# Cross-entropy backward on one core: the stores of second rows move from ACT's queue to Pool's

## The chip, the cores and the metric

The kernel runs on one core of a Trainium2 chip. Its engines work side by side and meet at semaphores: VectorE (DVE), ScalarE (ACT), GpSimd (Pool), SyncE (SP) and TensorE (PE). SP, ACT and Pool can issue DMAs; the data are moved by 16 DMA engines that all queues share. The metric is device time in microseconds, the median of the runs. The profile is of one further execution, and its span is the time from the first to the last instruction.

## The reference

For 8 x 1024 positions with 8192 logits each, the result is the softmax of the logits less 1.0 at the label:

```python
batch, seq_len, vocab = 8, 1024, 8192
logits_max = np.max(logits, axis=-1, keepdims=True)
exp_logits = np.exp(logits - logits_max)
softmax = exp_logits / np.sum(exp_logits, axis=-1, keepdims=True)
...
return (softmax - one_hot).astype(np.float32)
```

Input and output are 268.4 MB each in fp32; each is moved once.

## The kernel before

**Rows and blocks.** The 8192 positions are cut into T = 64 tiles of 128 positions, one to a partition; the code calls such a tile a row, t. A row is 128 x 8192 fp32, 32 KB on each partition, 4 MB. Two rows (G = 2) make a block, b = 0 to 31: row t = 2b is the block's first row (j = 0), t = 2b + 1 its second (j = 1). Both lie next to each other in memory on every partition. X holds SLOTS = 3 blocks, so block b uses slot b % 3, and everything is computed in place in X.

**Loads.** `load(b)` is called three blocks ahead. The string LOADS says in what pieces a block comes: "s" (blocks 0 to 2) in four half rows of 64 partitions, two of them on ACT's queue, "r" (blocks 3, 4 and 29 to 31) in two rows, "w" (blocks 5 to 28) as a whole block, 64 KB on each partition. All but the halves named are issued by SP. A load waits until the stores of block b - 3 that it would overwrite have landed: a row's load for that row's store, a block's load for both.

**One row.** `row_max(t)` on DVE (tensor_reduce, m) waits for the load. `exponentials(t)` on ACT takes exp and the sum s. `mark(t)`, two ACT operations, writes into PSUM (hot) a word that is 1 in the byte of the label. `finish(t)` on DVE takes the reciprocal r and then one scalar_tensor_tensor: X times r, less the bytes of hot. `store(t)` sends the row out. Each needs only what is named here, and `mark(t)` that `finish(t - 2)` has read hot.

**The order around a store.** It is written out by hand and is the same for all blocks. DVE does max(t1), finish(t0), max of the next block's first row, finish(t1). ACT does exp(t1), store(t0), mark(t0 + 2), exp of the next block's first row, store(t1), mark(t1 + 2). ACT executes its list in order, so an issue that waits for DVE holds what stands behind it. `store(t)` waits for DVE's count of `finish(t)`. All stores of blocks 0 to 30 are whole rows and are issued by ACT, each with a semaphore of its own for slot and row (`put`). The last block's two rows go out in halves of 4096 columns, row 62 by SP and row 63 by ACT. After the loop ACT waits for the landing of the last three blocks' stores.

**Pool** does four small fills, then an identity matrix and an iota for the marks, all at the start.

**Line numbers.** All instructions of the kernel are made by the helper `run` and have its line, L76 in the kernel before (L75 is its wait). In the changed kernel these are one more.

Of the kernel before, what the change touches and what calls it, by code (L numbers as in the profile page):

```python
# [9 lines left out]
SLOTS = 3  # L10
# [7 lines left out]
def kernel(  # L18
# [6 lines left out]
    nc = tc.nc  # L25
# [38 lines left out]
    with tc.tile_critical():  # L64
        sem = tc.alloc_semaphore
        got = [[sem(f"got{i}{q}") for q in range(4)] for i in range(SLOTS)]
        put = [[sem(f"put{i}{q}") for q in range(4)] for i in range(SLOTS)]
        lab_got, dve, act, pe, pool = (sem(n) for n in ("lab_got", "dve", "act", "pe", "pool"))
        count = {}

        def run(engine, waits, counter, method, **operands):

            waits = list(dict.fromkeys(waits))
            for w in waits[:-1]:
                engine.wait_ge(*w)  # L75
            instruction = getattr(engine, method)(**operands)  # L76
            for w in waits[-1:]:
                instruction._wait_ge(*w)
            step = 16 if method == "dma_start" else 1
            instruction.then_inc(counter, step)  # L80
            count[counter.name] = count.get(counter.name, 0) + step
            return counter, count[counter.name]
# [16 lines left out]
        maxed, summed, marked, finished, freed = {}, {}, {}, {}, {}  # L99
# [14 lines left out]
        def store(t):  # L114
            b, j = divmod(t, G)
            stored.setdefault(b, [])
            if t >= T - G:
                for i, cs in enumerate(sides):
                    w = run(
                        nc.sync if t == T - G else nc.scalar, [sides_done[t][i]], put[b % SLOTS][G * j + i],  # L120
                        "dma_start", out=o_b[b, every, one[j], cs], in_=X[every, b % SLOTS, one[j], cs],
                    )
                    stored[b].append(((every, one[j]), w))
                return
            for q, piece in enumerate(PIECES[STORES[b]]):
                ps, js = piece
                if js.stop != j + 1:
                    continue
                w = run(
                    nc.scalar, [finished[t]], put[b % SLOTS][q], "dma_start",  # L130
                    out=o_b[b, ps, js, :], in_=X[ps, b % SLOTS, js, :],
                )
                stored[b].append((piece, w))
# [110 lines left out]
        for b in range(B):  # L244
            t0, t1 = b * G, b * G + 1
            nxt = t1 + 1
            if ORDER[b] == "b":
                if t0 not in maxed:
                    row_max(t0)
                    exponentials(t0)  # L250
                row_max(t1)
                exponentials(t1)
                finish(t0)
                store(t0)
                mark(t0 + G)
                finish(t1)
                store(t1)
                mark(t1 + G)
                if b + SLOTS < B:
                    load(b + SLOTS)  # L260
                continue
# [4 lines left out]
            finish(t0)  # L266
            exponentials(t1)
            store(t0)
            mark(t0 + G)
            ahead = nxt < T and ORDER[b + 1] == "r"  # L270
# [42 lines left out]
```

## Time and profile before

| | |
|---|---|
| median of 3 runs | 1248.87 us (1248.83 to 1249.43) |
| span of the profiled execution | 1246.6 us |
| DVE busy | 1120.2 us |
| ACT busy | 722.7 us |
| Pool busy | 2.3 us |
| DVE idle, ended by a load | 105.4 us |
| HBM read, written | 268.50 MB, 268.44 MB |

In the profile an instruction's row gives its start and its time in us, the engine, the line, the operation and its tiles (out<-in). "ACTq" and "SPq" are the instructions with which ACT and SP issue DMAs; their time is that of the issue, and the transfer itself appears as a time to landing. Part 2 of the page cuts the span into 40 slices and gives busy shares in tenths. Part 3 gives for each DMA queue its packets, its megabytes and its share of the 16 engines' time: q10 is ACT's queue and q1 is SP's. A window is a stretch of the span with the busy time of each engine and the share of time that the DMA engines worked in it.

### The profile page before, as it was taken

How to read it: one execution, taken by the hardware profiler on the slowest of the kernel's cores; microseconds unless marked ns; L12 is line 12 of the kernel's file. 1: busy time of each engine (PE TensorE's matmuls, PEld its weight loads, DVE VectorE, ACT ScalarE, POOL GpSimd, SP SyncE). 2: the span in 40 equal slices, each digit the busy share in tenths (PEclk: the TensorE clock that was granted, in tenths of full speed). 3: DMA queues.
4: the chain of work that ended last, by engine and by line, in shares of the span. 5: the costliest groups of instructions: out<-in, count | busy, mean ns of one | idle time of the engine just before them, and what ended most of it. 6: DMA issues, size and time to landing. Idle time of an engine off the chain costs nothing.

```text
span 1246.6 us, 809 instructions
## 1 busy us (share of the span) xinstructions
PE 0.4 (0%) x2; PEld 0.3 (0%) x2; DVE 1120.2 (90%) x208; ACT 722.7 (58%) x257; POOL 2.3 (0%) x7
## 2 busy tenths in 40 slices
PE   0000000000000000000000000000000000000000
PEld 0000000000000000000000000000000000000000
DVE  5999998889988889888898888998889988899995
ACT  2866664556555565465655655556556555566662
POOL 0000000000000000000000000000000000000000
DMA  9999999999999999999999999999999999999998
GB/s 406 413 431 434 437 432 444 435 437 421 433 429 437 443 423 433 434 431 435 430 441 435 422 435 435 434 440 426 432 434 431 433 446 434 422 430 435 429 434 383
DMA packets 15413, 536.98 MB, mean 431 GB/s; under 512 B 1808, under 2 KB 1808, under 8 KB 1840
## 3 DMA queue, kind: packets, MB, share of 16 engines
q10 hardware_dynamic: 9744, 276.89, 51.5%
q1 hardware_dynamic: 5664, 260.05, 48.3%
q14 instruction: 5, 0.04, 0.0%
HBM read 268.50 MB, written 268.44 MB: 431 GB/s over the span
## 4 chain that ended last, share of the span: by engine, by line
DMA 59%; DVE 26%; issue 11%; ACT 3%; DVEq 0%; ACTq 0%; SPq 0%
DMA X<-in_logits_dram 33%; DMA out_dram<-X 26%; DVE X L76 15%; DVE m L76 10%; ACT X L76 2%; DVEq L64 0%; DVE r L76 0%; ACT hot L76 0%; ACT away L76 0%; ACTq L76 0%; DVEq L75 0%; ACTq L308 0%; SPq L64 0%
## 5 line engine op out<-in xcount | busy, mean ns | idle before, releaser
L76 ACT ACTIVATE X<-X,m 128x8192 f32<-128x8192 f32 x64 | 455.8, 7122 | 365.2 <-DVE m L76 365.2
L76 DVE TENSOR_REDUCE m<-X 128x1 f32<-128x8192 f32 x64 | 555.6, 8682 | 105.4 <-DMA X<-in_logits_dram 105.4
L76 DVE SCALAR_TENSOR_TENSOR X<-X,r,hot 128x8192 f32<-128x8192 f32 (+1 forms) x66 | 560.1, 8489 | 3.8 <-ACT hot L76 1.6
L76 ACT ACTIVATE away<-count,word 128x2048 bf16<-128x2048 int16 x64 | 128.1, 2001 | 127.0 <-DVE X L76 127.0
L76 ACT ACTIVATE hot<-away,unit,minus 128x2048 int32<-128x2048 bf16 x64 | 131.9, 2061 | 2.1
L76 ACT ACTIVATION_READ_ACCUMULATOR X<-X,m 128x1 f32 x64 | 11.9, 186 | 0.0
L76 DVE RECIPROCAL r<-s 128x1 f32<-128x1 f32 x64 | 9.8, 153 | 0.0
L76 ACT ACT_TABLE_LOAD x1 | 1.3, 1283 | 5.3 <-issue 5.3
L76 DVE CAST lab_f<-lab_raw 32x256 f32<-32x256 int32 x1 | 0.5, 536 | 2.7 <-DMA lab_raw<-in_labels_dram 2.7
L76 POOL IOTA count<- 128x2048 int16 x1 | 1.8, 1823 | 0.0
L76 DVE TENSOR_TENSOR unit<-unit,part 128x64 f32<-128x64 f32 x3 | 0.7, 225 | 0.1
L76 DVE CAST lab<-hot 128x64 int32<-128x64 f32 x1 | 0.2, 224 | 0.5 <-PE hot L76 0.5
L76 DVE TENSOR_SCALAR part<-minus 128x64 f32<-128x64 f32 x3 | 0.6, 194 | 0.1
L76 PE MATMUL hot<-ident,lab_f 32*128 32x32 f32 x2 | 0.4, 298 | 3.3 <-DVE lab_f L76 3.3
L76 PEld LDWEIGHTS hot<-ident,lab_f 32*128 32x128 f32 x2 | 0.3, 192 | 3.3 <-DVE lab_f L76 3.3
L76 DVE CAST minus<-lab 128x64 f32<-128x64 int32 x1 | 0.2, 195 | 0.0
L76 DVE TENSOR_SCALAR word<-part 128x64 f32<-128x64 int32 x1 | 0.2, 195 | 0.0
L76 DVE TENSOR_SCALAR lab<-lab 128x64 int32<-128x64 int32 x1 | 0.2, 195 | 0.0
L76 DVE TENSOR_SCALAR unit<-minus 128x64 f32<-128x64 f32 x1 | 0.2, 195 | 0.0
L76 DVE TENSOR_SCALAR part<-lab 128x64 int32<-128x64 int32 x1 | 0.2, 194 | 0.0
L76 DVE TENSOR_SCALAR minus<-unit 128x64 f32<-128x64 f32 x1 | 0.2, 194 | 0.0
L76 POOL TENSOR_SCALAR_AFFINE_SELECT ident<-ident 32x32 f32<-32x32 f32 x1 | 0.2, 203 | 0.1
(5 smaller groups left out, 0.5 us busy)
## 6 DMA issues: line engine op xcount, KB each, us to landing
out_dram<-X ACTq DMA_DIRECT2D x62, 4096.0 KB, 30.4
X<-in_logits_dram SPq DMA_DIRECT2D x10, 4096.0 KB, 28.1
X<-in_logits_dram SPq DMA_DIRECT2D x6, 2048.0 KB, 32.6
X<-in_logits_dram ACTq DMA_DIRECT2D x6, 2048.0 KB, 37.1
out_dram<-X SPq DMA_DIRECT2D x2, 2048.0 KB, 12.7
out_dram<-X ACTq DMA_DIRECT2D x2, 2048.0 KB, 11.9
X<-in_logits_dram SPq DMA_DIRECT2D x24, 33.4
lab_raw<-in_labels_dram ACTq DMA_DIRECT2D x1, 64.0 KB, 1.8
```

The source lines that it names most:

```text
L76: instruction = getattr(engine, method)(**operands)
```

## The change

A semaphore for each slot is added, and in `store` the full second rows (j = 1) of blocks 0 to 30 are issued by Pool, with that semaphore. Pool waits for `finish(t)` as ACT did. First rows stay on ACT, the last block's halves stay on SP and ACT. The loads and the final waits of ACT use whatever semaphore the store was given. Nothing else is edited; the order of all other instructions on every engine is the same.

```diff
@@ -65,6 +65,7 @@
         got = [[sem(f"got{i}{q}") for q in range(4)] for i in range(SLOTS)]
         put = [[sem(f"put{i}{q}") for q in range(4)] for i in range(SLOTS)]
+        second = [sem(f"second{i}") for i in range(SLOTS)]
         lab_got, dve, act, pe, pool = (sem(n) for n in ("lab_got", "dve", "act", "pe", "pool"))
@@ -127,7 +128,8 @@
                 w = run(
-                    nc.scalar, [finished[t]], put[b % SLOTS][q], "dma_start",
+                    nc.gpsimd if j else nc.scalar, [finished[t]], second[b % SLOTS] if j else put[b % SLOTS][q],
+                    "dma_start",
                     out=o_b[b, ps, js, :], in_=X[ps, b % SLOTS, js, :],
                 )
```

ACT's list loses 31 DMA issues, Pool's gains 31, each of 128 x 8192 fp32, behind the iota.

## The prediction

> **What bounds the kernel now.** The page's first parts: who is busy over the whole span, and what the DMA engines carry.
>
> ```profile
> span 1246.6 us, 809 instructions
> PE 0.4 (0%) x2; PEld 0.3 (0%) x2; DVE 1120.2 (90%) x208; ACT 722.7 (58%) x257; POOL 2.3 (0%) x7
> ...
> DMA  9999999999999999999999999999999999999998
> ...
> DMA packets 15413, 536.98 MB, mean 431 GB/s; under 512 B 1808, under 2 KB 1808, under 8 KB 1840
> ...
> q10 hardware_dynamic: 9744, 276.89, 51.5%
> q1 hardware_dynamic: 5664, 260.05, 48.3%
> q14 instruction: 5, 0.04, 0.0%
> ```
>
> DVE is 90% busy, but the DMA engines are busy in every slice: the two queues, ACT's q10 and SP's q1, fill 99.8% of them. How much is idle, and where, the windows say (columns: us; busy time of PE, PEld, DVE, ACT, POOL; clock; DMA share; GB/s):
>
> ```profile
> 0.00:2.30 2.30, 0.00 (x0) 0.00 (x0) 0.00 (x0) 0.00 (x0) 1.48 (x7) 1.00 0.09 29
> 160.00:1084.00 924.00, 0.00 (x0) 0.00 (x0) 827.16 (x142) 537.92 (x192) 0.00 (x0) 1.00 1.00 433
> 1084.00:1201.70 117.70, 0.00 (x0) 0.00 (x0) 117.15 (x21) 72.89 (x26) 0.00 (x0) 1.00 1.00 433
> 1201.70:1246.60 44.90, 0.00 (x0) 0.00 (x0) 31.32 (x8) 14.51 (x6) 0.00 (x0) 1.00 0.92 397
> ```
>
> From 160 to 1084 us DVE idles 97 of 924 us while the DMA share is 1.00 at 433 GB/s: DMA is the limit there. From 1084 us DVE has no gap (117.15 of 117.70) and DMA is still full. Both end together.
>
> A floor follows: 536.98 MB at 433 GB/s is 1240.1 us. Before it stand 2.3 us with no data; behind it stands what follows the last landing. That landing is read from the end of the timeline and the DMA view of the last stores (its last number is us from issue to landing):
>
> ```profile
> 1197.79 8.75 DVE L76 SCALAR_TENSOR_TENSOR X<-X,r,hot 128x8192 f32<-128x8192 f32 x1
> 1206.45 8.68 DVE L76 TENSOR_REDUCE m<-X 128x1 f32<-128x8192 f32 x1
> ...
> 1224.22 8.87 DVE L76 SCALAR_TENSOR_TENSOR X<-X,r,hot 128x4096 f32<-128x4096 f32 x2
> 1228.73 4.73 ACTq L76 DMA_DIRECT2D out_dram<-X  x2
> ...
> out_dram<-X ACTq DMA_DIRECT2D x2, 2048.0 KB, 11.9
> ```
>
> The last half store is issued at 1233.1 us (DVE's end, 1224.22 + 8.87), lands 11.9 us later at 1245.0, and 1.6 us remain. So 1240.1 + 2.3 + 1.6 = 1244.0 us, against a span of 1246.6. No order of issue can gain more than **2.6 us** unless bytes move faster. The median of the runs, 1248.87, lies 2.3 us above the span; I add 2.3 to every span below. 0.2% is 2.5 us, about what can be told from no change.
>
> **The change part by part.** (1) 31 second-row stores leave ACT's queue, each 0.34 us of issue (the row for 1171.67 below), 10.5 us in all. ACT is 58% busy, and behind such a store stands only the pair of marks for a row that is two rows (35 us) away: worth nothing. If ACT had no room it would be 10.5 us.
>
> (2) Pool issues them. It has 2.3 us of work, whose last and longest piece starts at 1.3 us and takes 1.8 (the row below), so it stands waiting for DVE when each row is done. Nothing but the next second-row store is queued behind that wait.
>
> (3) The semaphore of its own changes no order: SP's loads and ACT's last waits ask for the same landing under another name. Zero.
>
> (4) Pool's own price is in no row. From below: zero, since other transfers keep the engines in work while one starts. From above: all 16 engines standing still for the longest issue in the trace, 657 ns, at each of 31 stores, 20 us.
>
> The rows are those of the issues and of Pool's longest instruction, by tile (ns, shortest/median/longest):
>
> ```profile
> L76 SPq DMA_DIRECT2D X<-in_logits_dram x40: 327/328/657, 1.0 to 1173.0; - x40
> ...
> L76 POOL IOTA count<- x1: 1823/1823/1823, 1.3 to 1.3; 128x2048 int16 x1
> ```
>
> I take zero, the value for work hidden under full queues, and keep 20 us for the range.
>
> (5) The real change: **three queues instead of two share the engines.** How they share now can be read from packets, with the page's part 6 (DMA issues; the last number is us to landing):
>
> ```profile
> out_dram<-X ACTq DMA_DIRECT2D x62, 4096.0 KB, 30.4
> X<-in_logits_dram SPq DMA_DIRECT2D x10, 4096.0 KB, 28.1
> X<-in_logits_dram SPq DMA_DIRECT2D x6, 2048.0 KB, 32.6
> X<-in_logits_dram ACTq DMA_DIRECT2D x6, 2048.0 KB, 37.1
> out_dram<-X SPq DMA_DIRECT2D x2, 2048.0 KB, 12.7
> ...
> X<-in_logits_dram SPq DMA_DIRECT2D x24, 33.4
> lab_raw<-in_labels_dram ACTq DMA_DIRECT2D x1, 64.0 KB, 1.8
> ```
>
> Every DMA ends in 16 small packets: with the two of 11.9 us above these are 113 DMAs, and 113 x 16 = 1808, the "under 512 B". Without these and the 5 of q14, 13,600 are left, which is the number of partition rows that these DMAs move, one packet each (62 x 128 for the stores, 24 x 128 for the block loads, and so on): 32 KB for a row's store or load, 64 KB for a block's load. And the queues take turns, packet by packet, as two neighbouring row loads in the tail show, each with its issue and its time to landing:
>
> ```profile
> 1153.66 0.33 SPq L76 DMA_DIRECT2D X<-in_logits_dram  x1
> X<-in_logits_dram SPq DMA_DIRECT2D x1, 4096.0 KB, 28.5
> ...
> 1173.00 0.33 SPq L76 DMA_DIRECT2D X<-in_logits_dram  x1
> X<-in_logits_dram SPq DMA_DIRECT2D x1, 4096.0 KB, 28.7
> ```
>
> They land at 1182.2 and 1201.7, 19.5 us apart. One row is 4.19 MB, 9.69 us at 433 GB/s; 19.5 is twice that: load and store alternate one to one. With a second store queue that has work, a row load gets a third. In the middle of the kernel this costs nothing: engines that are full stay full, and what loads lose stores gain. But stores run ahead of loads, and at the end that is the wrong way round: stores are what DMA does beside DVE's last rows.
>
> ```profile
> 1171.67 0.34 ACTq L76 DMA_DIRECT2D out_dram<-X  x1
> out_dram<-X ACTq DMA_DIRECT2D x1, 4096.0 KB, 34.8
> ...
> 1189.12 0.34 ACTq L76 DMA_DIRECT2D out_dram<-X  x1
> ```
>
> When the last load lands (1201.7), the store of 1171.67 has 4.8 us to go (it lands at 1206.5) and that of 1189.12 its full 9.69: a stock of 14.5 us, 1.5 rows. DVE was 4.75 us late for that load (its reduce starts at 1206.45): it is not waiting.
>
> How short may the way from the last landing be? DVE 1206.45 to 1233.09, 26.64 us; then the last two half stores, 9.68 us in a row, the first of which starts 4.43 us before DVE's end, so 5.25; start and landing 1.8, the time of the smallest DMA (lab_raw in part 6); and the 1.6 us after it: **35.3 us**. Before, that way takes 44.9 us, so 9.6 us of cushion; the stock pays for it.
>
> With two store queues a store starts as soon as its row is done. Alone beside a load it takes 19.4 us, and rows come 17.45 us apart (1171.67 to 1189.12), so 1.11 are under way, half done on the mean: 0.56 rows of stock. If the three always share, 29 us: 0.83. I take 0.7. The 0.8 rows that are gone were stored ahead of loads, 0.8 x 9.69 = 7.75 us. In each 17.45 us by which the last load is late, DVE adds another row that is stored ahead of it too, so the delay is 7.75 / (1 - 9.69/17.45) = 7.75 / 0.445 = 17.4 us. The last load lands at 1219.1, and the span is 1219.1 + 35.3 = 1254.4 us. With +2.3: **1256.7 us**. (At stock 0.83 it is 1254, at 0.56 it is 1260. It takes DVE's pace as unbroken in the tail; where DVE waits for loads the delay is a little smaller.)
>
> **Rivals.** *Not slower: Pool starts late, so the stock stays.* From stock 1.06 on, the delay is under the cushion of 9.6 us and nothing is lost: 1249. On the mean of all rows, stock grows by d/(2 x 17.45) for a start d us late, so 0.36 more needs d of 12.6 us. For it: what Pool needs to start a 4 MB store is unknown. Against: its longest instruction is 1.8 us. The Trainium skill, "SBUF — State Buffer", section "SBUF: two separate sides", says that a DVE operation in a two-port mode keeps Pool from writing descriptors; its section "Who interferes with whom" says that tensor_reduce never does. By the first, at the 8.75 us of DVE's longest operation (1197.79), the stock would be 0.95 and the time 1251. No run here shows which holds.
>
> *Faster.* First rows no longer queue behind second rows, slots come free sooner, and the 2.6 us above the floor vanish: 1246.3 at best. Against: engines that are full cannot use an earlier issue.
>
> *Slower still: Pool's packets are pieces of a row.* Then Pool's turn is small beside the load's 64 KB, the second-row store waits for the block load that shares the engines, and SP's next load waits for that store. From there each of 24 block loads begins with queues nearly dry for a start and landing, 1.8 us: 43 us, 1292. For it: SP has nothing to issue until stores land, in most of the kernel:
>
> ```profile
> SPq L76 <- DMA out_dram<-X: 644.9, 34, 67.9
> SPq L75 <- DMA out_dram<-X: 511.1, 24, 21.6
> ```
>
> Against: all packets of SP and ACT are whole rows.
>
> *A lump.* If Pool's turn is several rows, second rows go at nearly full speed but first rows and loads stand behind them: stock near 0.9, delay 0.6 x 9.69 / 0.445 = 13.1 us, span 1201.7 + 13.1 + 35.3 = 1250.1, time 1252. The Trainium skill, "DMA: Bandwidth & Descriptors", section "Queues, rings and completion order", says that an engine drains a whole packet of typically 9 to 17 descriptors before it switches queues. That would be this case; the packets counted above are single rows.
>
> **How the numbers follow.** Even sharing at no price of Pool's, 1254 to 1260: 52%. A lump, 1250 to 1254: 11%. Even sharing and a price of Pool's up to the 20 us of (4), 1260 to 1277: 8%. Late start, 1249: 12%. Pieces, 1292: 13%. Faster: 4%. The prediction is the first, 1256.7. The range must give up 2 in 10: the pieces, the gain and the lowest part of the late starts, hence 1249 to 1277. Faster than 1246.4: 0.04. Within 0.2%: the late starts and the low part of the lump, 0.14. Slower: 0.82.
>
> **What would show it.** Right: Pool's queue with 31 x 128 packets of 32 KB; the DMA share 1.00 until some 1200 us with the middle unchanged in GB/s; the last row load landing 10 to 20 us later than 1201.7; DVE waiting for loads in the tail, where it now waits for none; a dip of DMA before the last stores; second-row landings near 20 to 29 us. Wrong: if the DMA share falls below 1.00 in the middle (pieces, or a price at each store); if bytes per packet of q1 and q10 stay but the packets' time grows; if the last load lands before 1211 and the time is still up.

## The result and the profile after

The changed kernel takes **1287.49 us** (6 runs, 1278.49 to 1294.59) against 1248.83 us before (6 runs, 1248.63 to 1249.43): ratio 1.030, 95% interval 1.0266 to 1.0333. That is 38.7 us slower, where 8 were forecast, and above the forecast range of 1249 to 1277. The runs also scatter by 16 us, those before by 0.8.

The page of the changed kernel, with the rows that answer to those shown of before (part 5's row of Pool's issues is new):

```profile
span 1284.7 us, 809 instructions
...
DMA  9999999899999999999999999999999999999978
GB/s 395 424 437 420 402 410 426 337 422 426 437 432 434 417 435 425 425 440 421 425 426 436 437 426 423 426 435 438 439 424 419 423 426 430 422 414 405 410 309 359
...
q1 hardware_dynamic: 5664, 260.05, 47.9%
q10 hardware_dynamic: 5280, 146.87, 26.7%
q0 software_dynamic: 4464, 130.03, 23.9%
...
L77 POOL DMA_DIRECT2D out_dram<-X x31 | 16.6, 536 | 1230.2 <-DVE X L77 1230.2
...
out_dram<-X ACTq DMA_DIRECT2D x31, 4096.0 KB, 22.2
out_dram<-X POOLq DMA_DIRECT2D x31, 4096.0 KB, 29.9
X<-in_logits_dram SPq DMA_DIRECT2D x10, 4096.0 KB, 46.8
...
X<-in_logits_dram SPq DMA_DIRECT2D x24, 31.5
```

Pool's queue is q0. Its 4464 packets are 31 x (128 + 16): one packet for each partition's row and 16 small ones for each store, the same packets as on ACT's queue. Bytes and packets in all are those of before. What grew is the time the same packets take, and the time in which there were none. A queue's share times the span is its time on the 16 engines. Loads (q1): 0.483 x 1246.6 = 602.1 us before, 0.479 x 1284.7 = 615.4 now, **13.3 more**. Stores (q10 and q0, with the few loads that ACT issues at the start): 642.0 before, 650.1 now, **8.1 more**. What is left of the span is DMA idle time: 2.5 us before, 19.3 now, **16.8 more** (0.1% of share is 1.3 us). The sum is 38.2, and the span grew by 38.1.

The windows of the changed kernel (columns as before):

```profile
160.00:1084.00 924.00, 0.00 (x0) 0.00 (x0) 807.54 (x139) 523.28 (x185) 12.22 (x23) 1.00 1.00 425
1084.00:1201.70 117.70, 0.00 (x0) 0.00 (x0) 107.04 (x19) 72.50 (x28) 2.12 (x4) 1.00 1.00 412
1201.70:1284.70 83.00, 0.00 (x0) 0.00 (x0) 61.49 (x13) 29.77 (x10) 0.53 (x1) 1.00 0.84 352
```

The DMA share still reads 1.00 where 433 GB/s became 425 and 412: **busy engines that move less**. Only the GB/s column tells it. Then the issue and the landing of two loads, the last whole block (block 28) and the last row:

```profile
1077.28 0.33 SPq L77 DMA_DIRECT2D X<-in_logits_dram  x1
X<-in_logits_dram SPq DMA_DIRECT2D x1, 30.9
...
1201.26 0.33 SPq L77 DMA_DIRECT2D X<-in_logits_dram  x1
X<-in_logits_dram SPq DMA_DIRECT2D x1, 4096.0 KB, 47.2
```

Block 28 lands at 1108.2; before, DVE starts on it at 1084.3, right as it lands. So 24 us are lost by there. The last row lands at 1248.5 instead of 1201.7, 46.8 us later: the other 23 are lost in the tail. From there to the end it is 1284.7 - 1248.5 = 36.2 us; the prediction had 35.3 for this way. But it is not the last row that DVE waits for:

```profile
DVE m L77 <- DMA X<-in_logits_dram: 147.8, 28, 17.2
...
1231.59 8.69 DVE L77 TENSOR_REDUCE m<-X 128x1 f32<-128x8192 f32 x1 [9.42 <-DMA X<-in_logits_dram]
...
1249.05 8.68 DVE L77 TENSOR_REDUCE m<-X 128x1 f32<-128x8192 f32 x1
```

In all DVE waits 147.8 us for loads, 42.4 more than before. The last of these waits, 9.42 us, ends with the landing of row 62. Row 63, the last one, lands 0.6 us before DVE is free for it at 1249.05. Both reductions start 42.6 us later than before (there at 1189.00 and 1206.45).

### The profile page after: what moved, and what is told of

Read it like the earlier page. It is cut to its first block, busy times and chain, and to the rows that moved or that the text cites. A ratio compares the mean times of both kernels' runs of the same rounds, so it can differ in the third digit from the quotient of the medians.

```text
span 1284.7 us, 809 instructions
## 1 busy us (share of the span) xinstructions
PE 0.4 (0%) x2; PEld 0.3 (0%) x2; DVE 1120.4 (87%) x208; ACT 722.7 (56%) x257; POOL 18.9 (1%) x38
## 3 DMA queue, kind: packets, MB, share of 16 engines
q0 software_dynamic: 4464, 130.03, 23.9%
## 4 chain that ended last, share of the span: by engine, by line
DMA 65%; DVE 19%; issue 11%; ACT 3%; another core or an unknown queue 1%; DVEq 0%; ACTq 0%; SPq 0%
DMA X<-in_logits_dram 36%; DMA out_dram<-X 30%; DVE X L77 13%; DVE m L77 6%; ACT X L77 2%; DVEq L64 0%; DVE r L77 0%; ACT hot L77 0%; ACT away L77 0%; ACTq L77 0%; DVEq L76 0%; ACTq L310 0%; SPq L64 0%
## 5 line engine op out<-in xcount | busy, mean ns | idle before, releaser
L77 DVE TENSOR_REDUCE m<-X 128x1 f32<-128x8192 f32 x64 | 555.6, 8682 | 147.8 <-DMA X<-in_logits_dram 147.8
L77 POOL DMA_DIRECT2D out_dram<-X x31 | 16.6, 536 | 1230.2 <-DVE X L77 1230.2
## 6 DMA issues: line engine op xcount, KB each, us to landing
X<-in_logits_dram SPq DMA_DIRECT2D x10, 4096.0 KB, 46.8
```

## Experiments

Below, "loads", "stores" and "idle" are engine time taken as above. "Empty starts" counts, from the issue and landing times of every store between 70 and 1180 us, how often a store was issued to a queue in which no store was left; before it is 0, in the changed kernel 28 of 29 on ACT and 27 of 28 on Pool. "Together" is the time in which both store queues have a store between its issue and its landing, for stores issued up to 1180 us.

**1. All whole-row stores through Pool.** Two queues again; Pool carries 62 stores.

```diff
-                    nc.gpsimd if j else nc.scalar, [finished[t]], second[b % SLOTS] if j else put[b % SLOTS][q],
+                    nc.gpsimd, [finished[t]], second[b % SLOTS][j],
```

> All 62 whole-row stores go through Pool, none through ACT: Pool's queue carries twice as many stores, but there are again only two queues, and a row's store never runs beside another's. Theory A (two streams): what costs is that two rows' stores run at once, which makes packets slower and lets the 16 engines fall out of step; then this is back near the time before, 1246 to 1255 us, with row packets at 1.21 us and little spread at the landings. Theory B (Pool's path): every store through Pool costs, some 38.7/31 = 1.25 us; then 62 of them make about 1326 us.

1250.34 us, ratio 1.0017 (1.0008 to 1.0027). From its page:

```profile
span 1248.8 us, 809 instructions
...
q1 hardware_dynamic: 5664, 260.05, 48.4%
q0 software_dynamic: 8928, 260.05, 48.3%
q10 hardware_dynamic: 816, 16.84, 3.2%
...
out_dram<-X POOLq DMA_DIRECT2D x62, 4096.0 KB, 30.0
```

Loads take 604.4 us of the engines, stores 643.1: the values before. Pool's path is not the cause; 62 stores through it cost 2.2 us in all, where theory B had 1326 us.

**2. Second rows on SP.**

```diff
-                    nc.gpsimd if j else nc.scalar, [finished[t]], second[b % SLOTS] if j else put[b % SLOTS][q],
+                    nc.sync if j else nc.scalar, [finished[t]], second[b % SLOTS] if j else put[b % SLOTS][q],
```

> Second rows are issued by SP instead of Pool: no work for Pool, two queues, and second-row stores stand in one queue with the loads while first-row stores run on ACT's. Theory A (two streams): two stores still run at once, though with two turns instead of three; some of the loss stays, above 1258 us, and slow store packets show. Theory B (Pool's path): without Pool the loss is gone, 1246 to 1255 us.

1344.28 us, ratio 1.0764 (1.0746 to 1.0781): far above both the 1258 us that theory A had as the least and the range of theory B. Part 6 says why:

```profile
out_dram<-X ACTq DMA_DIRECT2D x31, 4096.0 KB, 24.4
out_dram<-X SPq DMA_DIRECT2D x31, 4096.0 KB, 42.1
...
X<-in_logits_dram SPq DMA_DIRECT2D x24, 24.3
```

A second-row store now stands in SP's queue behind a block's load (24.3 us to landing), and the next load waits for its landing, 42.1 us after its issue (a load goes out every 42.4 us); the 16.8 MB that a block moves take 38.7 us at 433 GB/s. So each block takes longer than its transfers should. This mixes a new wait with the loss in question and decides nothing between A and B. Packets do take longer here without Pool: the queues' shares add up to 0.964 of the span, 0.964 x 1338.7 = 1290.5 us of engine time against 1244.1 before, 46.4 more, with no DMA issued by Pool. But by the packet records 24 of the 34 loads after the start begin here while no other packet is under way, against 1 of 34 in the changed kernel, so these long packets need not be those of the change (experiment 9 has the same).

**3 and 4. Pool in the middle alone, and at the ends alone.** In one, Pool issues the second rows of blocks 6 to 25; in the other those of blocks 0 to 5 and 26 to 30. ACT issues the rest.

```diff
-                    nc.gpsimd if j else nc.scalar, [finished[t]], second[b % SLOTS] if j else put[b % SLOTS][q],
+                    nc.gpsimd if j and 6 <= b < 26 else nc.scalar, [finished[t]],
+                    second[b % SLOTS] if j and 6 <= b < 26 else put[b % SLOTS][q],
```

> Pool issues the second rows of blocks 6 to 25 alone (20 stores, all beside whole-block loads); at both ends ACT issues them as before. If the loss arises at the ends, beside row loads (packets of 32 KB), this is 1249 to 1258 us. If every store through Pool costs the same, 1249 + 20 x 1.25 = 1274 us.

> Pool issues the second rows of blocks 0 to 5 and 26 to 30 alone (11 stores, most of them beside row loads). If the loss arises at the ends, 1272 to 1287 us. If every store through Pool costs the same, 1249 + 11 x 1.25 = 1263 us. The prediction's own term (the tail's stock of stores) would give 1254 to 1260 us.

The middle: 1257.43 us, ratio 1.0097 (1.006 to 1.0133), in runs from 1251.0 to 1266.2. The ends: 1275.08 us, ratio 1.022 (1.0198 to 1.0242). 20 stores cost 9 us, 11 cost 27: not a price per store. Two thirds of the loss arises at the two ends, where the row loads are; whether it is the row loads that do it, 6 and 7 ask.

**5. Three queues with two of loads.** The kernel before, with the loads of odd blocks from 3 on issued by Pool.

```diff
+                on_pool = b >= SLOTS and b % 2 == 1
                 w = run(
-                    queue, free, got[b % SLOTS][q], "dma_start",
+                    nc.gpsimd if on_pool else queue, free, other[b % SLOTS][q] if on_pool else got[b % SLOTS][q], "dma_start",
```

> The kernel before, with all stores on ACT, but the loads of odd blocks from block 3 on are issued by Pool: three queues again, now two with loads and one with stores. Theory A1 (any third queue): three queues in work at once make packets long and set the engines apart; then the ends lose again, above 1260 us, with packets over 1.3 us in the row-load phases. Theory A2 (two store streams): only two rows' stores at once do it; then 1246 to 1255 us and packets of 1.21 us.

1249.51 us, ratio 1.0008 (0.9998 to 1.0017). Engine time in all 0.998 x 1247.9 = 1245.4, as before (1244.1). A second queue of loads costs next to nothing. As a test of a third queue it is weak: of the transfers issued from 62 to 1180 us, all three queues had one under way together for 42 us, against 283 us in the changed kernel. At the change's loss for each such microsecond these 42 would cost 6 us (an estimate, 38.7 x 42/283); 1.1 were measured.

**6 and 7. Whole-block loads everywhere, with and without the change.**

```diff
-LOADS = "sssrrwwwwwwwwwwwwwwwwwwwwwwwwrrr"
+LOADS = "ssswwwwwwwwwwwwwwwwwwwwwwwwwwwww"
```

> The changed kernel, but all blocks from 3 on are loaded whole (64 KB packets), also at the two ends. To be read against the next run, which has these loads without the change. Theory R (row loads): the long store packets need loads with packets of the same 32 KB, so that the three queues run in equal steps; then the two runs are within 10 us. Otherwise the difference stays at 25 us or more.

> The kernel before with all blocks from 3 on loaded whole; the control for the run above. All theories: loads wait for both stores of a slot and DVE for both rows, which costs something at the ends; 1250 to 1275 us, no long packets.

With the change 1272.15 us (1262.8 to 1280.1), without it 1257.45. The change costs 14.7 us here instead of 38.7: between the two branches. Row loads make it worse, but are not needed.

**8. Pool waits for the first row's landing.**

```diff
-                    nc.gpsimd if j else nc.scalar, [finished[t]], second[b % SLOTS] if j else put[b % SLOTS][q],
+                    nc.gpsimd if j else nc.scalar, [finished[t]] + ([stored[b][0][1]] if j else []),
+                    second[b % SLOTS] if j else put[b % SLOTS][q],
```

> The changed kernel, but Pool's store of a second row also waits until the store of the first row of the same block has landed. A second row still runs beside the next block's first row, but less often are two stores under way. Theory A (stores side by side beside loads): the loss shrinks by half or more, 1249 to 1268 us. If the loss came from Pool's starts or from ACT's queue running dry, no better than the change, 1280 us or more.

1281.37 us, ratio 1.027 (1.0234 to 1.0307): no repair. But the edit hardly did what it was made for: the time together is 413 us, against 463 us in the changed kernel. So it does not speak against theory A. Each queue started from empty 28 times.

**9. One store at a time.** All whole rows through Pool as in the first, each waiting for the landing of the one before.

```diff
+                    nc.gpsimd, [finished[t]] + ([stored[b - 1 + j][-1][1]] if t else []), second[b % SLOTS][j],
```

> All whole-row stores go through Pool, as in the first experiment, and each waits until the row's store before it has landed: never two stores under way, but the store queue runs empty after every one, while loads go on. Theory D (the store queue runs empty): what costs is a store that starts on an empty queue beside a running load; then packets are long here too and the time is above 1265 us. Theory A (two rows' stores at once): 1249 to 1260 us, packets at their usual 1.21 and 2.42 us.

1415.46 us, ratio 1.1336 (1.1319 to 1.1352). Its page, and the first row of its waits:

```profile
span 1410.9 us, 870 instructions
...
q1 hardware_dynamic: 5664, 260.05, 46.1%
q0 software_dynamic: 8928, 260.05, 42.8%
q10 hardware_dynamic: 816, 16.84, 2.8%
...
POOL out_dram L77 <- DMA out_dram<-X: 1311.5, 61, 32.5
```

Loads take 0.461 x 1410.9 = 650.4 us of the engines, 48 more than before; stores 643.4, as before. Idle is 117 us. Most of the time lost is idling between landings and starts, which this experiment brings in by itself.

The time is above theory D's 1265 us, but the packet records show another mechanism. All 34 loads after the start begin here when a store has just landed and no other packet is under way. Of the 128 packets of each block load, the first 32 (two for each of the 16 engines) took 3.15 us on the mean and the other 96 their usual 2.42, although stores started on an empty queue beside them. All 431 long ones are among the first 32. So the 48 us belong to loads that start on idle engines. In the changed kernel only one load starts so, and of the 12 us by which its block loads exceed the median packet time, 8 lie behind the first 32 packets.

**10. Each row stored in two halves of 64 partitions, one by ACT and one by Pool.**

```diff
+            for ps in halves:
+                on_pool = ps == halves[1]
                 w = run(
-                    nc.gpsimd if j else nc.scalar, [finished[t]], second[b % SLOTS] if j else put[b % SLOTS][q],
+                    nc.gpsimd if on_pool else nc.scalar, [finished[t]],
+                    second[b % SLOTS][j] if on_pool else put[b % SLOTS][j], "dma_start",
```

> Every whole row is stored in two halves of 64 partitions at once, one by ACT and one by Pool: two store queues work at the same time, always on the same row. Theory A (two store queues beside the loads): the loss is there again, above 1265 us, with long packets. If it needs two different rows, whose 32 KB pieces lie next to each other in memory and whose stores start at different times: 1248 to 1260 us.

1320.8 us, ratio 1.0576 (1.0559 to 1.0594). The loss does not need two different rows. It also does not need queues that are mostly empty: here the time together is 1096 us, and a store found its queue empty 18 times of 54 on ACT and 15 of 54 on Pool, against 28 of 29 and 27 of 28 in the changed kernel. Yet the engine time is 0.978 x 1320.0 = 1291.0 us, 46.9 more than before, where the change added 21.4. (Each transfer is half a row here, which no run separates.)

**11. The roles of Pool and SP exchanged.** Pool issues the loads from block 3 on, SP the second-row stores.

```diff
-                    queue, free, got[b % SLOTS][q], "dma_start",
+                    nc.gpsimd if b >= SLOTS else queue, free, other[b % SLOTS][q] if b >= SLOTS else got[b % SLOTS][q], "dma_start",
...
-                    nc.gpsimd if j else nc.scalar, [finished[t]], second[b % SLOTS] if j else put[b % SLOTS][q],
+                    nc.sync if j else nc.scalar, [finished[t]], second[b % SLOTS] if j else put[b % SLOTS][q],
```

> The changed kernel with two roles exchanged: Pool issues the loads from block 3 on, SP the second-row stores, ACT the first-row stores. Three queues, two of them with stores, and neither store queue is Pool's. Theory A (two store queues): as long as the change, 1270 to 1295 us. If Pool's kind of queue is needed for the loss when it carries one of two stores: 1247 to 1258 us.

1285.39 us, ratio 1.0305 (1.0251 to 1.036): the time of the change, with no store on Pool. Theory A's range is met. Part 6 has the change's picture under other names:

```profile
out_dram<-X ACTq DMA_DIRECT2D x31, 4096.0 KB, 20.3
out_dram<-X SPq DMA_DIRECT2D x31, 4096.0 KB, 28.5
```

**12. The kernel before with row loads everywhere.**

```diff
-LOADS = "sssrrwwwwwwwwwwwwwwwwwwwwwwwwrrr"
+LOADS = "sssrrrrrrrrrrrrrrrrrrrrrrrrrrrrr"
```

> The kernel before with all blocks from 3 on loaded in rows (32 KB packets), all stores on ACT, no Pool: loads get half of the turns beside a store instead of two thirds. Theory D (the store queue runs empty): stores now keep up with DVE in the middle too; if the one store queue runs empty, packets get long and the time is above 1253 us. Theory A (two stores at once): there is one store stream, so no long packets and 1246 to 1252 us.

1248.76 us, ratio 1.0004 (0.9995 to 1.0014). Both theories could live with it, since the store queue did not run empty: the stores' median to landing went up to 51.8 us, not down. Row loads alone do no harm.

**13. Two stores under way.** As 9, but each store waits for the one before the one before it.

```diff
+                    nc.gpsimd, [finished[t]] + ([stored[b - 1][j][1]] if b else []), second[b % SLOTS][j],
```

> All whole-row stores through Pool, each waiting for the landing of the store before the one before it: a dose of the earlier run in which each waited for the one just before. One store is always queued behind the one that runs, so the queue should not run empty while DVE keeps up. Theory D: back at the time without any such wait, 1248 to 1258 us, load packets at 2.42 us. If the wait on a landing itself costs (rather than the empty queue): at least a third of the earlier run's loss, above 1300 us.

1250.59 us, ratio 1.0019 (1.001 to 1.0029). Page and waits:

```profile
span 1247.9 us, 869 instructions
...
q1 hardware_dynamic: 5664, 260.05, 48.4%
q0 software_dynamic: 8928, 260.05, 48.3%
...
POOL out_dram L77 <- DVE X L77: 1136.6, 60, 41.9
```

All of Pool's waits but two are ended by DVE now, not by landings, the queue never runs empty, no load starts on idle engines, and loads are back at 604.0 us. One store queued behind the one that runs is enough.

**14. The changed kernel with row loads everywhere** (the edit of 12 on it).

> The changed kernel (second rows on Pool) with all blocks from 3 on loaded in rows, as in the run before with one store queue, where stores took 51.8 us to land and the store queue always held more than two rows. Theory D (empty store queue): if both store queues keep work, packets stay at 1.21 us and the time is 1249 to 1260 us. Theory A (two stores at once beside row loads): the long store packets seen at the ends now come all the time, above 1290 us.

1297.05 us, ratio 1.0398 (1.0381 to 1.0415): above theory A's 1290 us.

```profile
span 1293.7 us, 809 instructions
...
q1 hardware_dynamic: 9120, 260.05, 47.5%
q10 hardware_dynamic: 5280, 146.87, 27.1%
q0 software_dynamic: 4464, 130.03, 23.9%
...
X<-in_logits_dram SPq DMA_DIRECT2D x58, 4096.0 KB, 55.6
out_dram<-X ACTq DMA_DIRECT2D x31, 4096.0 KB, 25.0
out_dram<-X POOLq DMA_DIRECT2D x31, 4096.0 KB, 27.0
```

Here a store is under way at every moment from 70 to 1180 us, so the stores as a whole never stop; yet each of the two queues starts from empty 28 times, and loads (614.5) and stores (659.8) are both long. A pause of all stores, as in 9, is therefore not needed. Two store queues that stay filled all the time were not reached; experiment 10 comes nearest, and it loses most of all kernels with two store queues but 2.

The packets that start after 72 us (the loads of the start left out), counted from the trace's packet records; the last column is how many took over 1.3 times the median:

```
kernel   queue and size          number  median   mean  longest (ns)  over 1.3x
before   ACT stores      32 KB     7799    1213   1213     1611           1
before   SP block loads  64 KB     3072    2418   2422     3321           1
after    ACT stores      32 KB     3865    1213   1222     2192          42
after    Pool stores     32 KB     3929    1213   1238     2464         112
after    SP block loads  64 KB     3072    2418   2479     3860          53
1        Pool stores     32 KB     7801    1213   1214     1668           1
1        SP block loads  64 KB     3072    2418   2426     3260           2
9        Pool stores     32 KB     7808    1213   1217     1332           0
9        SP block loads  64 KB     3072    2418   2601     3782         431
14       ACT stores      32 KB     3872    1213   1250     2427         162
14       Pool stores     32 KB     3930    1213   1245     2760         143
14       SP row loads    32 KB     7424    1213   1236     2731         187
```

The medians never move. A few packets take up to twice their time or more and carry much of what the means gain. Long **store** packets go with two store queues in this table (after, 14; not 9). In 6, with two store queues and whole-block loads, the stores stay under 1.6 us and 164 of 3712 load packets are long.

Experiment 3 is a caution. Its profiled run was the fastest of its four (1251.0 us, the others 1257.2 to 1266.2). In it all 20 of Pool's stores and 21 of 38 on ACT started from empty, and yet no packet took over 1.3 times its median. So a start from empty does not by itself make packets long, and the same kernel does not lose the same time in every run.

## Why the prediction was wrong, point by point

**Right.** The bound: the DMA engines were full and no time was to be had from ACT's issue. (1) to (3), issue and semaphore: nothing. (4), Pool's price, taken as zero: its issue is 536 ns on the mean, 16.6 us in all on an idle engine, and 62 such stores cost 2.2 us. So nothing shows here of what the Trainium skill says of DVE keeping Pool from writing descriptors ("SBUF — State Buffer", "SBUF: two separate sides"). That is no test of it, since 29 of the 31 issues ran beside a tensor_reduce and the other two beside no DVE instruction. A start 12.6 us late is not seen either: 62 stores on Pool's queue land 30.0 us after issue, those on ACT's 30.4. The packet is one partition's row on Pool's queue too, so the "lump" is out, and so are the "pieces": that rival's 1292 us lies near the result by luck, not by its mechanism. Right are also the direction, DVE's waits in the tail, and the time from the last row's landing to the end (36.2 us for 35.3), though DVE had only just come free for that row.

**Wrong, in step (5).** It said that in the middle "this costs nothing: engines that are full stay full, and what loads lose stores gain". The engines stayed full by the share and moved 425 instead of 433 GB/s, which over these 924 us is 17 us of transfers. The step took the time of a packet as fixed, 9.69 us per row whatever else runs. In the changed kernel 21.4 us on the mean of the engines went into packets that took longer, and landings wait for the slowest of the 16 engines: of the last row's load the first engine was done at 1231.3 us and the last at 1248.5, 17 us apart, where before these were 3.0 us apart. From there come the late loads, DVE's waits in the tail and the 16.8 us of idle. It is one of the signs of being wrong that the prediction itself had named: the bytes per packet stay and the packets' time grows.

**Mis-sized with it: the delay of the last load.** The stock of stores was to put it off by 17.4 us; it was 46.8, of which 24 were there before the tail began, where the step had put nothing. The stock itself was mis-sized too: when the last load lands, no store is under way (the last one landed at 1246.1, the next is issued at 1249.4), where 0.7 rows were forecast. How much of the other 23 us is stock and how much long packets, no run separates.

**What the runs show in its place.** A packet's time is not fixed, and it grows when the stores have two queues. The loss comes with the second store queue (the change, 3, 4, 6, 8, 10, 11, 14), whichever engines issue the stores (11), and not with Pool (1, 13) or row loads (12). All five kernels besides the one before that have one store queue which never runs empty (1, 5, 7, 12, 13) have 1245 to 1248 us of engine time; of the 9 us that 7 loses most are idle (10.0 us of it, 2.5 before).

**What stays open.** The runs do not say what it is about the second store queue. That it does its harm by running empty is not shown: 10 has fewer empty starts and twice the extra engine time, 3 had 41 empty starts and almost no loss in its profiled run, and 9 and 2 are slow in another way, by loads that start on idle engines. Two stores under way at once on two queues fit the kernels named better (1096 us of it in 10, 463 in the change), but so do three queues at work at once, which 5 had for 42 us only. Why a packet takes up to twice its time is not shown by any run.

The Trainium skill, "DMA: Bandwidth & Descriptors", section "Rules for kernel authors", says that spreading DMAs over SP, ACT and GpSimd does not help bandwidth. Here it did worse than not help: 425 for 433 GB/s in the middle, and 3.0% of the time.

## What to carry to other kernels

Where the DMA engines were full, a second queue of stores took nothing off them, and their packets took longer. Keep one queue of stores with at least one more always waiting behind the one that runs (13 against 9), and judge the engines by their GB/s and by engine time (share times span), not by a busy share of 1.00. When a move between queues is costed, a packet's time is a term of its own and can grow.

## What was not expected of the hardware

- A load that starts while no other packet is under way begins with long packets: in experiment 9 the first 32 of a block load's 128 packets took 3.15 us on the mean, the others 2.42. Stores lost almost nothing there (643 us in all, 642 before).
- With two store queues the 16 engines drift apart within one transfer: up to 41.5 us between the first and the last engine's completion of one 4 MB load in experiment 14 and 19 us in the changed kernel, against 3.0 us at most before.
- A store on Pool's queue is nearly as good as one on ACT's: 62 of them land 30.0 us after issue against 30.4, at 0.54 us of issue against 0.34, and cost 2.2 us in all.
- Second-row stores on SP's own queue, behind the loads, cost 96 us (experiment 2): more than a second store queue beside ACT's in any other experiment (72 us at most, in 10).
